# A decoder trunk on one core: scaled activations issued earlier, one more pair of columns with seven products in each gated MLP, and other times for the sums in DRAM

## The chip, the core and the metric

The kernel runs on one core of a Trainium2 chip. TensorE multiplies matrices and writes its results to PSUM; VectorE (DVE), ScalarE (ACT) and GpSimd (POOL) do the elementwise work; SyncE (SP) issues most DMA transfers, GpSimd the adding ones. Every engine has its own instruction stream, executed in the order in which the program lists it; the engines wait for one another on semaphores. The metric is the time of one execution on the device in microseconds. The kernel before took 1473.97 us (median of 3 runs, 1472.92 to 1474.12).

## The reference

One batch of 512 positions of width 1024 passes through two layers. Each layer has a mixer (layer 0: a gated short convolution beside differential attention; layer 1: stick-breaking attention), a cross-attention into 256 memory tokens, and a gated MLP. All of it is in float32. The change touches the gated MLP, shown here with its norm:

```python
def rmsnorm(x, g):
    xf = x.astype(jnp.float32)
    y = xf * lax.rsqrt(jnp.mean(xf * xf, axis=-1, keepdims=True) + EPS)
    return (y * g.astype(jnp.float32)).astype(x.dtype)

def conv_ffn(h, w_up, w_conv, w_down):
    """Gated MLP with causal depthwise width-3 conv between up-projection and activation."""
    u = causal_dwconv(h @ w_up, w_conv)
    gate, val = jnp.split(u, 2, axis=-1)
    return (jax.nn.silu(gate) * val) @ w_down

# in every layer l
x = x + conv_ffn(rmsnorm(x, norm_ffn[l]), ffn_w_up[l], ffn_conv[l], ffn_w_down[l])
```

`w_up` is 1024 x 5632 (2816 gate columns and 2816 value columns), `w_down` 2816 x 1024.

## The kernel before

Activations lie transposed, 128 features on the partitions by 512 positions, so the width of 1024 is eight chunks. Every float32 operand of a product is carried as two parts, `hi` (rounded) and `lo` (the remainder), and a product is three matmuls: hi x hi, hi x lo and lo x hi. The helper `split` makes the parts: a copy on ScalarE for `hi`, a subtraction on VectorE for `lo`.

Weights come in groups (`weight_groups`), loaded in order by SP (`loads`, `halved_loads`) into three `raw` buffers, and are split (`prep`, `prep_halved`) into five `hi` and five `lo` buffers. For groups in `LOW` the low part is made otherwise: ScalarE writes the negated rounded weights and a DMA issued by GpSimd adds the weights to them (`add_dma`).

The up-projection goes in 22 pairs `U0` to `U21`: 128 gate columns with the 128 value columns that belong to them. The order of pairs and of the parts of the down-projection is `FFN_ORDER`: U0 to U7, then D(0,0), U8, D(0,1), U9, U10 and so on; U13, U14, U15 and U16 follow one another.

- Pairs below `UP_SCALED` = 6 multiply activations that carry the norm's gain but not yet its per-position factor; their results are scaled when they leave PSUM (`up_done`: a multiplication by `rrow`), because the factor is known only later.
- Pairs from 6 on use the scaled activations that `fold` (line 1467) makes once `rrow` is known: four quarters, each with two scaled chunks (`N["S"]`) and their sums and differences (`N["T"]`).
- A plain pair is 8 chunks x 2 halves x 3 matmuls of 512 columns. A pair in `SEVEN` (line 40) is computed by `lin_halved` (line 804) as a 2 x 2 block product with seven block products in place of eight: 7 x 4 x 3 matmuls of 256 columns, with sums of the weight blocks before and sums of the products afterwards, on VectorE. Each product goes through the four quarters of the fold in turn.

The sums of the weight blocks for pairs in `SUMMED` (line 42) are made in DRAM by `sums_in_dram` (line 658): SP copies the group of 1 MB within DRAM, then GpSimd issues three adding DMAs, each of which waits for the one before. The table names, for each pair, the group after whose end the sum is spawned. `halved_loads` then loads the pair's four tiles `a`, `d`, `b` and `c`, two of them from DRAM sums.

Every result passes through `done` streams: evacuation from PSUM, `conv3` (line 1154: one ScalarE pass and two VectorE steps), the activation, the product of gate and value, and the split for the down-projection.

The order of every engine's instructions is fixed when the program is written, by a planner (`Issue.run`, line 337). Each piece of work is a stream with a priority (a lower number goes first). The planner keeps a modelled time for every engine, takes the engine on which something can start first, and among the streams that can start there at that time picks the one of the lowest number. The priorities that matter here: 0.5 for the norm's chunks, `SUM` (line 151) for the norm's sums of squares, 1.0 for the `done` streams, `FOLD` (line 153, used in line 1585) for the fold, 3.0 for the preparation of weights, 6.0 for the sums in DRAM, 10 and up for the matmuls. Fixed numbers of buffers bound how far a stream can run ahead: three PSUM accumulators (`acc`), two each of `sc` and `tr` and one `pv`, six `c` buffers in SBUF.

Of the kernel before, what the change touches and what calls it, by code (L numbers as in the profile page):

```python
# [36 lines left out]

UP_SCALED = 6
FFN_ORDER = [('u', 0), ('u', 1), ('u', 2), ('u', 3), ('u', 4), ('u', 5), ('u', 6), ('u', 7), ('d', 0, 0), ('u', 8), ('d', 0, 1), ('u', 9), ('u', 10), ('d', 0, 2), ('u', 11), ('u', 12), ('d', 0, 3), ('u', 13), ('u', 14), ('u', 15), ('u', 16), ('d', 1, 0), ('u', 17), ('d', 1, 1), ('u', 18), ('d', 1, 2), ('u', 19), ('u', 20), ('d', 1, 3), ('u', 21), ('d', 2, 0), ('d', 2, 1)]
SEVEN = {0: (7, 8, 9, 10, 11, 12, 13, 14, 15, 16, 17, 18, 19, 20, 21), 1: (7, 8, 9, 10, 11, 12, 13, 14, 15, 16, 17, 18, 19, 20, 21)}  # L40

SUMMED = {0: {7: 'A1', 8: 'A1', 9: 'A2', 10: 'A2', 11: 'EO0', 12: 'EO0', 13: 'EO1', 14: 'KV1_0', 15: 'KV3_0', 16: 'Q0_0', 17: 'Q0_0', 18: 'Q1_0', 19: 'XO0_0', 20: 'XO0_0', 21: 'XO1_0'}, 1: {7: 'U17_0', 8: 'U19_0', 9: 'U21_0', 10: 'SQK0', 11: 'SQK0', 12: 'SV0', 13: 'SQK1', 14: 'SQK2', 15: 'SV1', 16: 'SQK3', 17: 'Q0_1', 18: 'Q1_1', 19: 'XO0_1', 20: 'XO1_1', 21: 'U1_1'}}


def weight_groups():
# [57 lines left out]
GROUPS = weight_groups()  # L103
GN = {g[0]: i for i, g in enumerate(GROUPS)}

LOW = {GN[n] for n in ('U2_0', 'U2_1', 'U3_0', 'U3_1', 'U4_0', 'U4_1', 'U5_0', 'U5_1', 'U6_0', 'U6_1')}
LOW7 = {GN[n] for n in ()}
ADDED = {GN[f"U{j}_{l}"]: GN[after] for l in SUMMED for j, after in SUMMED[l].items()}
HALVED = {GN[f"U{j}_{l}"] for l in SEVEN for j in SEVEN[l]}
NSLOT = [len(g[3]) * len(g[4]) * P // SLOT for g in GROUPS]  # L110
# [37 lines left out]

POW_WAIT = 0.0

PREP_FIRST, SUM_FIRST, SUM = 0.45, 3.2, 1.5

FOLD = 1.4

SUMS = 6.0
PE_RATE, PE_FIX = 2400.0, 0.0133
# [88 lines left out]
class Issue:  # L245
# [8 lines left out]
    def spawn(self, gen, prio):  # L254
        self.seq += 1
        self.streams.append(Stream(gen, prio, self.seq))
# [133 lines left out]
def trunk(ctx: ExitStack, tc: tile.TileContext, xT: bass.AP, memT: bass.AP, wts: bass.AP, par: bass.AP, outT: bass.AP):  # L390
# [36 lines left out]
    def act(out, in_, func=AF.Copy, scale=1.0, bias=None, accum=None):  # L427
        out, in_ = vw(out), vw(in_)
        scale, bias, accum = vw(scale), vw(bias), vw(accum)
        d = (0.051 if in_.psum() else 0.093) + in_.n() / 1200.0  # L430
        d += 0.093 * (isinstance(scale, V) + (bias is not None)) + 0.2 * (accum is not None)
        kw = {}
        if bias is not None:
            kw["bias"] = _raw(bias)
        if accum is not None:
            kw["accum_out"] = _raw(accum)
        if func == AF.Copy and scale is not None and not isinstance(scale, V) and scale == 1.0:
            def fn():
                return nc.scalar.copy(out=out.ap, in_=in_.ap)  # L439
        else:  # L440
            def fn():
                return nc.scalar.activation(out=out.ap, in_=in_.ap, func=func, scale=_raw(scale), **kw)  # L442
        return Op("ACT", d, [in_, scale, bias], [out, accum], fn)
# [299 lines left out]
    def prep(groups):  # L743
        for gi in groups:
# [3 lines left out]
            for s in range(NSLOT[gi]):  # L748
# [9 lines left out]
                else:  # L758
                    yield Until(lambda: (gi, s) in raws)
                    raw = raws[gi, s]  # L760
                    yield act(hi, raw)
                    if gi in LOW:
                        yield act(lo, raw, scale=-1.0)
# [699 lines left out]
    def ffn(l, xin, xout, last):  # L1463
# [40 lines left out]
        def up_done(j):  # L1504
            def done(m, ps):
                gate = m % 2 == 0
                u = ps
                if j < UP_SCALED:
                    u = yield AL(pC)
                    yield Until(lambda: "rrow" in N)  # L1510
                    yield tt(u, ps, N["rrow"], ALU.mult)
                    free(ps)
                t = yield AL(pG)
                yield from conv3(u, f"ffn_conv{l}", j if gate else 22 + j, 44, t)
                free(u)
                if gate:
                    yield act(t, t, AF.Silu)
                    gate_t[j] = t
                    F["silu", l] = F.get(("silu", l), 0) + 1
                else:  # L1520
                    yield Until(lambda: j in gate_t)
                    yield tt(t, t, gate_t[j], ALU.mult)
                    free(gate_t[j])
                    if 4 <= j < 16 or j > 19:
                        q = pHS if j < 16 else pG
                        hi, lo = yield [AL(q, F32R), AL(q, F32R)]
                        o, w = (hi, lo), (hi, lo)
                    else:
                        y = yield AL(pH, F32R, (P, 2, S))
                        o, w = (y[:, 0, :], y[:, 1, :]), (y,)  # L1530
                    yield from split(o[0], o[1], t)
                    free(t)
                    own[j] = w
                    acts[j] = o
            return done

        def up(j):
            done = up_done(j)
            if j in SEVEN[l]:
                acc = yield AL(aACC)  # L1540
# [43 lines left out]

        spawn(fold(), FOLD)
        for step in FFN_ORDER:
# [283 lines left out]
```

## Time and profile before

| what | before |
|---|---|
| median of 3 runs | 1473.97 us |
| profiled execution | 1473.73 us |
| its span, first to last instruction | 1471.9 us |
| TensorE busy | 1465.0 us |
| VectorE / ScalarE / GpSimd busy | 1113.1 / 810.7 / 168.5 us |
| moved by DMA | 243.41 MB |

The span lies 1.83 us below the profiled execution's time. The profile's matmuls overlap and their ends are modelled, so the distance between two starts tells how long one takes, not its duration. "Idle before" is the time in which an engine had nothing to execute just before an instruction, and the arrow names what ended it. A DMA's time to landing runs from its issue to the last byte. In the trace `L492` is the helper that records matmuls, `L454` the one for elementwise work on two tensors, `L439` and `L442` ScalarE's copies and activations, `L462` VectorE's scaled additions, `L501` SP's DMAs and `L508` the adding DMAs of GpSimd (POOL).

### The profile page before, as it was taken

The numbers are of one execution on the slowest core, as the hardware profiler recorded it, in microseconds if no ns is written. First come the engines' busy times: TensorE is split into PE (matmuls) and PEld (weight loads), VectorE is DVE, ScalarE is ACT, GpSimd is POOL, SyncE is SP. The second block draws the span as 40 slices with busy tenths as digits, with TensorE's granted clock in tenths as the row PEclk, the third lists the DMA queues.
The fourth block names the chain that finished last, engine by engine and source line by source line (L and its number), as shares of the span: only waits on it lengthen the run. The fifth ranks groups of instructions, "written<-read, shape, count | busy, mean of one in ns | idle before, by whom it ended". The sixth has DMA issues, their size and how long they took to land.

```text
span 1471.9 us, 21459 instructions
## 1 busy us (share of the span) xinstructions
PE 1465.0 (100%) x8048; PEld 1272.2 (86%) x8048; DVE 1113.1 (76%) x1891; ACT 810.7 (55%) x1335; POOL 168.5 (11%) x249
## 2 busy tenths in 40 slices
PE   9999999999999999999999999999999999999998
PEld 8888888888889999999888888888888889999897
DVE  7689766665798788867687989967656996888683
ACT  6576546453675445444477877855535854545341
POOL 3212121211210000000111111001101300000000
PEclk9999999999999999999999999999999999999999
DMA  6128898967784445658465463453547954455351
GB/s 237 58 86 243 224 264 269 255 169 161 178 177 143 144 151 170 200 169 227 158 154 147 122 187 79 137 178 107 148 126 219 224 149 128 144 159 184 117 165 57
DMA packets 86088, 243.41 MB, mean 165 GB/s; under 512 B 8064, under 2 KB 8576, under 8 KB 85504
## 3 DMA queue, kind: packets, MB, share of 16 engines
q1 hardware_dynamic: 63744, 200.09, 40.2%
q0 software_dynamic: 22240, 41.95, 17.6%
q8 instruction: 63, 1.03, 0.3%
q14 instruction: 41, 0.34, 0.1%
HBM read 239.91 MB, written 65.01 MB: 207 GB/s over the span
## 4 chain that ended last, share of the span: by engine, by line
PE 95%; DVE 2%; ACT 2%; DMA 1%; issue 1%; SPq 0%; DVEq 0%; ACTq 0%
PE acc L492 67%; PE sc L492 13%; PE pv L492 6%; PE tr L492 6%; PE tr L496 3%; DVE lo L454 0%; ACT h L439 0%; DMA raw<-wts 0%; ACT g L442 0%; DMA x<-xT 0%; DVE g L1619 0%; DVE h L454 0%; DVE g L454 0%; DVE c L454 0%; ACT pt L439 0%
## 5 line engine op out<-in xcount | busy, mean ns | idle before, releaser
L492 PE MATMUL acc<-hs,hi 128*128 128x512 f32 x1568 | 493.7, 392 | 0.0
L439 ACT CAST hi<-raw 128x1024 fp32r<-128x1024 f32 (+1 forms) x294 | 303.3, 1038 | 211.1 <-PE acc L492 79.8
L454 DVE TENSOR_TENSOR lo<-raw,hi 128x1024 fp32r<-128x1024 f32 (+1 forms) x274 | 328.7, 1205 | 90.7 <-ACT hi L439 89.5
L492 PEld LDWEIGHTS acc<-hs,hi 128*128 128x128 f32 x1568 | 292.4, 188 | 57.7
L492 PE MATMUL acc<-hs,lo 128*128 128x512 f32 x784 | 307.5, 392 | 0.0
L492 PE MATMUL acc<-hi,hs 128*128 128x512 f32 x544 | 175.4, 395 | 0.3 <-ACT hs L442 0.3
L492 PEld LDWEIGHTS acc<-hs,lo 128*128 128x128 f32 x784 | 147.3, 188 | 28.7
L492 PE MATMUL acc<-h,hi 128*128 128x512 f32 (+1 forms) x600 | 170.2, 368 | 0.0
L454 DVE TENSOR_TENSOR x<-x,acc 128x512 f32<-128x512 f32 (+1 forms) x105 | 71.2, 680 | 71.4 <-PE acc L492 71.1
L492 PEld LDWEIGHTS acc<-h,hi 128*128 128x128 f32 x600 | 108.2, 189 | 18.1
L462 DVE SCALAR_TENSOR_TENSOR g<-c,pp,g 128x511 f32<-128x511 f32 (+1 forms) x168 | 116.9, 745 | 2.5 <-ACT g L442 2.4
L492 PEld LDWEIGHTS acc<-hi,hs 128*128 128x128 f32 x544 | 100.9, 188 | 20.3 <-ACT hs L442 0.6
L492 PE MATMUL acc<-h,lo 128*128 128x512 f32 (+1 forms) x300 | 109.5, 368 | 0.0
L492 PE MATMUL acc<-lo,hs 128*128 128x512 f32 x272 | 106.8, 393 | 0.0
L492 PE MATMUL acc<-y,hi 128*128 128x512 f32 (+1 forms) x280 | 74.2, 346 | 0.0
L508 POOL DMA_DIRECT2D dr<-wts x30 | 27.4, 913 | 392.1 <-DMA dr<-wts 385.6
L442 ACT ACTIVATE g<-c,pp 128x512 f32<-128x512 f32 x84 | 58.1, 719 | 19.1 <-DVE c L454 18.9
L454 DVE TENSOR_TENSOR g<-g,g 128x512 f32<-128x512 f32 (+2 forms) x112 | 62.9, 568 | 5.0 <-ACT g L439 2.0
L492 PEld LDWEIGHTS acc<-h,lo 128*128 128x128 f32 x300 | 56.6, 189 | 9.4
L442 ACT ACTIVATE g<-sc,rq 128x128 f32<-128x128 f32 (+7 forms) x128 | 61.2, 537 | 5.4 <-PE sc L492 4.9
L508 POOL DMA_DIRECT2D dr<-dr x60 | 50.3, 848 | 115.3 <-DMA dr<-wts 70.1
L492 PEld LDWEIGHTS acc<-lo,hs 128*128 128x128 f32 x272 | 51.2, 188 | 10.0
(241 smaller groups left out, 2672.1 us busy)
## 6 DMA issues: line engine op xcount, KB each, us to landing
raw<-wts SPq DMA_DIRECT2D x226, 512.0 KB, 4.2
raw<-dr SPq DMA_DIRECT2D x60, 512.0 KB, 3.7
dr<-wts POOLq DMA_DIRECT2D x30, 512.0 KB, 6.1
dr<-dr POOLq DMA_DIRECT2D x60, 256.0 KB, 4.7
lo<-wts POOLq DMA_DIRECT2D x20, 512.0 KB, 7.8
raw<-wts SPq DMA_DIRECT2D x38, 256.0 KB, 3.1
x<-xT SPq DMA_DIRECT2D x16, 256.0 KB, 4.7
raw<-memT SPq DMA_DIRECT2D x4, 512.0 KB, 4.5
```

The costliest lines, as they stand in the source:

```text
L439: return nc.scalar.copy(out=out.ap, in_=in_.ap)
L442: return nc.scalar.activation(out=out.ap, in_=in_.ap, func=func, scale=_raw(scale), **kw)
L454: lambda: _ve(eng).tensor_tensor(out=out.ap, in0=in0.ap, in1=in1.ap, op=op))
L462: lambda: nc.vector.scalar_tensor_tensor(out=out.ap, in0=in0.ap, scalar=_raw(scalar), in1=in1.ap, op0=op0, op1=op1))
L492: lambda: nc.tensor.matmul(out.ap, lhsT.ap, rhs.ap, start=start, stop=stop))
L496: return Op("PE", 0.109, [in_, ident_v], [out], lambda: nc.tensor.transpose(out.ap, in_.ap, ident_v.ap))
L508: lambda: nc.gpsimd.dma_start(out=out.ap, in_=i, accum_op=ALU.add, max_dma_last_dim=2048))
```

## The change

Three things change, by tables and priorities alone; no function is edited.

- Pair 6 of both layers joins `SEVEN` and leaves `LOW`. It needs a sum in DRAM too, so it enters `SUMMED`: 32 sums in place of 30.
- The fold's priority goes from 1.4 to 0.8 and the norm sums' from 1.5 to 0.7, so both stand ahead of the `done` streams at 1.0.
- The sums in DRAM are spawned after other groups. Layer 0's pairs 18 to 21 come after pairs 7 to 10 of the first gated MLP; layer 1's pairs 6 to 14 after its pairs 11 to 20; layer 1's last four after pairs 8 to 11 of the second gated MLP. None is spawned in the stick-breaking layer.

```diff
 UP_SCALED = 6
-SEVEN = {0: (7, 8, 9, 10, 11, 12, 13, 14, 15, 16, 17, 18, 19, 20, 21), 1: (7, 8, 9, 10, 11, 12, 13, 14, 15, 16, 17, 18, 19, 20, 21)}
-SUMMED = {0: {7: 'A1', 8: 'A1', 9: 'A2', 10: 'A2', 11: 'EO0', 12: 'EO0', 13: 'EO1', 14: 'KV1_0', 15: 'KV3_0', 16: 'Q0_0', 17: 'Q0_0', 18: 'Q1_0', 19: 'XO0_0', 20: 'XO0_0', 21: 'XO1_0'}, 1: {7: 'U17_0', 8: 'U19_0', 9: 'U21_0', 10: 'SQK0', 11: 'SQK0', 12: 'SV0', 13: 'SQK1', 14: 'SQK2', 15: 'SV1', 16: 'SQK3', 17: 'Q0_1', 18: 'Q1_1', 19: 'XO0_1', 20: 'XO1_1', 21: 'U1_1'}}
+SEVEN = {0: (6, 7, 8, 9, 10, 11, 12, 13, 14, 15, 16, 17, 18, 19, 20, 21), 1: (6, 7, 8, 9, 10, 11, 12, 13, 14, 15, 16, 17, 18, 19, 20, 21)}
+SUMMED = {0: {6: 'A1', 7: 'A1', 8: 'A2', 9: 'A2', 10: 'EO0', 11: 'EO0', 12: 'EO1', 13: 'KV1_0', 14: 'Q0_0', 15: 'Q0_0', 16: 'Q1_0', 17: 'XO0_0', 18: 'U7_0', 19: 'U8_0', 20: 'U9_0', 21: 'U10_0'}, 1: {6: 'U11_0', 7: 'U12_0', 8: 'U13_0', 9: 'U14_0', 10: 'U15_0', 11: 'U16_0', 12: 'U17_0', 13: 'U18_0', 14: 'U20_0', 15: 'Q0_1', 16: 'Q1_1', 17: 'XO0_1', 18: 'U8_1', 19: 'U9_1', 20: 'U10_1', 21: 'U11_1'}}
...
-LOW = {GN[n] for n in ('U2_0', 'U2_1', 'U3_0', 'U3_1', 'U4_0', 'U4_1', 'U5_0', 'U5_1', 'U6_0', 'U6_1')}
+LOW = {GN[n] for n in ('U2_0', 'U2_1', 'U3_0', 'U3_1', 'U4_0', 'U4_1', 'U5_0', 'U5_1')}
...
-PREP_FIRST, SUM_FIRST, SUM = 0.45, 3.2, 1.5
-FOLD = 1.4
+PREP_FIRST, SUM_FIRST, SUM = 0.45, 3.2, 0.7
+FOLD = 0.8
```

## Prediction

> **What bounds the kernel now.** I read the page first, then the busy time by stretch, then the starts of the matmuls. Lines of the page of before: the span, the busy time of TensorE, the chain that ended last, and the issues of plain weight loads.
>
> ```profile
> span 1471.9 us, 21459 instructions
> ...
> PE 1465.0 (100%) x8048; PEld 1272.2 (86%) x8048; DVE 1113.1 (76%) x1891; ACT 810.7 (55%) x1335; POOL 168.5 (11%) x249
> ...
> PE 95%; DVE 2%; ACT 2%; DMA 1%; issue 1%; SPq 0%; DVEq 0%; ACTq 0%
> ...
> L454 DVE TENSOR_TENSOR lo<-raw,hi 128x1024 fp32r<-128x1024 f32 (+1 forms) x274 | 328.7, 1205 | 90.7 <-ACT hi L439 89.5
> ...
> raw<-wts SPq DMA_DIRECT2D x226, 512.0 KB, 4.2
> ```
>
> TensorE is on the chain for 95% of the span and idle for 6.9 us of it (1471.9 - 1465.0). Every microsecond that its instruction stream loses is therefore won, and every wait that it gains is lost. Where the 6.9 us lie, by stretch (busy time of each engine, number of instructions, clock, DMA share, GB/s):
>
> ```profile
> core 0: us, PE busy (x) PEld busy (x) DVE busy (x) ACT busy (x) POOL busy (x), PEclk, DMA share, GB/s
> 110.00:160.00 50.00, 49.47 (x256) 41.50 (x255) 42.68 (x122) 28.60 (x68) 12.43 (x13) 1.00 0.85 217
> 211.00:254.00 43.00, 43.00 (x201) 35.51 (x200) 29.56 (x42) 24.60 (x43) 7.32 (x9) 1.00 0.85 260
> 390.00:440.00 50.00, 50.00 (x222) 41.38 (x222) 46.20 (x78) 37.05 (x53) 8.42 (x7) 1.00 0.85 187
> 440.00:500.00 60.00, 60.00 (x372) 54.26 (x371) 44.70 (x67) 28.61 (x39) 0.00 (x0) 1.00 0.40 128
> 740.00:800.00 60.00, 59.31 (x298) 49.53 (x297) 48.23 (x79) 42.53 (x85) 11.06 (x29) 1.00 0.65 160
> 800.00:850.00 50.00, 49.68 (x262) 41.30 (x261) 49.25 (x83) 43.76 (x86) 8.13 (x28) 1.00 0.43 114
> ```
>
> TensorE has no gap at all where the first gated MLP begins (390 to 500 us), at the full granted clock (1.00). What gaps the change could remove lie in 110:160 (0.53 us) and in the stick-breaking layer, 740:800 and 800:850 (0.69 + 0.32 us). Most of the rest stands at the start and the end of the span. So the change can win little except by shortening the stream itself.
>
> **The change part by part.** *Pair 6 with seven products.* Starts of matmuls on TensorE (start, us busy, what, count), at the borders of steps of both gated MLPs:
>
> ```profile
> 440.39 0.62 PE L492 MATMUL acc<-y,hi 128*128 128x512 f32 x2
> ...
> 451.27 0.40 PE L492 MATMUL acc<-y,hi 128*128 128x256 f32 x2
> ...
> 461.34 0.63 PE L492 MATMUL acc<-h,hi 128*128 128x512 f32 x2
> ...
> 585.58 0.40 PE L492 MATMUL acc<-y,hi 128*128 128x256 f32 x2
> ...
> 1185.88 0.62 PE L492 MATMUL acc<-y,hi 128*128 128x512 f32 x2
> ...
> 1196.76 0.40 PE L492 MATMUL acc<-y,hi 128*128 128x256 f32 x2
> ...
> 1206.83 0.63 PE L492 MATMUL acc<-h,hi 128*128 128x512 f32 x2
> ```
>
> The plain pair 6 runs from 440.39 to 451.27, 10.88 us for its 48 matmuls (2 halves x 8 chunks x 3) of 512 columns: 227 ns each. Pair 7, already with seven products, runs from 451.27 to 461.34, 10.07 us for 84 matmuls (7 x 4 x 3) of 256 columns: 120 ns each. Layer 1 has the same differences (1196.76 - 1185.88 and 1206.83 - 1196.76). The edit turns one 10.88 into a 10.07 in each layer: 2 x 0.81 = **1.62 us less**, all on the path.
>
> The Trainium skill ("TensorE: Matmul & The Clock Gate", section Back-to-back issue gap) gives a sustained 81 ns per matmul of 128 columns and 131 ns of 512; an estimate on the line between them is 98 ns for 256, by which 84 x 98 = 8.2 us would replace 48 x 131 = 6.3 us and each pair would lose 1.9 us. The trace disagrees with both figures (227 and 120 ns), so the measured difference stands.
>
> *What pair 6 costs on the other engines.* So far its low parts are made by ScalarE and an adding DMA; now VectorE makes them: three of 1.2 us (the page's row) and a half one, and it also combines the products with seven sums. Rows of VectorE in pair 7's turn:
>
> ```profile
> 457.56 0.69 DVE L454 TENSOR_TENSOR sq<-raw,sq 128x512 fp32r<-128x512 f32 x1
> ...
> 461.55 0.42 DVE L454 TENSOR_TENSOR c<-sc,c 128x256 f32<-128x256 f32 x1
> 461.88 0.41 DVE L454 TENSOR_TENSOR c<-c,sc 128x256 f32<-128x256 f32 x1
> ```
>
> That is 3 x 1.2 + 0.7 + 7 x 0.33 = 6.6 us more of VectorE per layer. In 440:500 VectorE is idle for 60 - 44.70 = 15.3 us, which hides it; the results are wanted only when the down projection that starts at 461.34 reaches its seventh and eighth chunk. I take nothing; were the cover gone, it would cost up to 6.6 us in each layer. ScalarE trades four passes over 1024 columns for three and two small ones: nothing. POOL loses two adding DMAs for low parts, and SP issues four loads in place of two.
>
> *The fold.* The scaled activations (`fold`) get priority 0.8, ahead of the 1.0 of the evacuations and convolutions of pairs 0 to 5. Pair 6 needed only the plain scaled chunks, one after another; with seven products its first product needs all four quarters, the last some 1.1 us after its start (three quarters of a 1.44 us product, 10.07 / 7), at about 441.5. Where each quarter starts now on VectorE, and its last write:
>
> ```profile
> 390.70 0.74 DVE L462 SCALAR_TENSOR_TENSOR c<-x,pp,rrow 128x512 f32<-128x512 f32 x1
> ...
> 409.63 1.41 DVE L462 SCALAR_TENSOR_TENSOR c<-x,pp,rrow 128x512 f32<-128x512 f32 x2
> ...
> 422.46 0.74 DVE L462 SCALAR_TENSOR_TENSOR c<-x,pp,rrow 128x512 f32<-128x512 f32 x1
> ...
> 435.98 1.40 DVE L462 SCALAR_TENSOR_TENSOR c<-x,pp,rrow 128x512 f32<-128x512 f32 x2
> ...
> 449.68 0.68 DVE L454 TENSOR_TENSOR rrow<-c,pt 128x512 fp32r<-128x512 f32 x1
> ```
>
> It ends at 450.36, 0.9 us before pair 7; for the new pair 6 that is 8.9 us late. The quarters take 18.9, 12.8, 13.5 and 14.4 us, though a quarter has only some 5 us of VectorE work (two scalings of 0.7, four low parts of 0.7, four sums of 0.4: 5.8 by durations). What stretches them is the pairs' work between, which the new priority puts behind. Bounds: at 5.8 us each the fold ends at 414; at 12.8 each it ends at 442, just late. I take an end near 425, so **nothing**. The displaced work is two scaled copies and four convolution steps a pair, held by the three accumulators and six `c` buffers; VectorE has 3.8 us of idle time in 390:440, so the backlog is pushed into the 15.3 us after 440.
>
> The norm sums (`SUM`, 0.7) move ahead of the same evacuations: one addition of about 0.7 us in front of another, neither of them last before the statistics. I take nothing.
>
> *The sums in DRAM.* 32 in place of 30. By stage, before and after: even layer and first cross-attention 15 and 12; first gated MLP 3 and 13; stick-breaking layer 7 and 0; second cross-attention 4 and 3; second gated MLP 1 and 4. So the stick-breaking layer loses its traffic. Its largest gap, at 779.38, goes back to a weight load. From the chain of waits (start, us, what), the waits of ScalarE and of POOL's queue, and the gap:
>
> ```profile
> 769.95 6.26 DMA raw<-wts
> ...
> 776.23 1.05 ACT L439 CAST hi<-raw 128x1024 fp32r<-128x1024 f32 x1 [2.72 <-DMA raw<-wts]
> ...
> 769.09 0.89 POOL L508 DMA_DIRECT2D dr<-wts  x1 [9.18 <-DMA dr<-wts]
> ...
> 779.38 0.55 PE tr L496 x3
> ...
> PE tr L496 <- DVE pt L454: 0.7, 1, 0.7
> ```
>
> The load took 6.26 us against the page's median of 4.2, beside a sum's add that POOL issued at 769.09; ScalarE held a copy and the cast of `pt` behind it. Without the sum it comes up to 2.1 us earlier, more than the 0.7 us that TensorE waited. Bounds: 0 (another operand is late next) and 1.0 (all the idle time of both stretches). I take **0.7 us less**.
>
> Sum, against the profiled execution's own time (1473.73, of which 1.83 lie outside its span): 1473.73 - 1.62 - 0.7 = 1471.4. The median of the runs is 0.24 above that execution: **1471.7**. If the 0.7 stays, 1472.4.
>
> **The rivals.** *Slower: the first gated MLP becomes bound by its weight loads (0.22).* Loads of the dense stretch as they are, and a stretch with one sum (queue: packets, MB, share; then the issues with KB and median time to landing):
>
> ```profile
> q1 hardware_dynamic: 3880, 8.41, 55.1%
> ...
> raw<-wts SPq DMA_DIRECT2D x8, 512.0 KB, 3.7
> ...
> q0 software_dynamic: 560, 1.05, 21.2%
> ...
> raw<-wts SPq DMA_DIRECT2D x7, 512.0 KB, 5.7
> ```
>
> The first two rows are of 560:610, the others of 660:692. Loads: 55.1% of 50 us for 8.41 MB is 3.28 us of all DMA engines per MB; a pair of 3.5 tiles (1.84 MB) needs 6.0 us. A sum: its adds 21.2% of 32 us = 6.8 us, its 1.05 MB copy 3.4 us. With a sum after every pair a pair's time of 10.07 us meets 16.2 us of DMA. Pairs 13 to 16 follow each other without a down projection: 4 x 6.1 = 24.5 us too much. Against that stands the lead of the weights, as here (cast and its low part on VectorE; the product that uses them starts at 585.58):
>
> ```profile
> 575.19 1.05 ACT L439 CAST hi<-raw 128x1024 fp32r<-128x1024 f32 x1 [1.18 <-DMA raw<-wts]
> 577.18 1.22 DVE L454 TENSOR_TENSOR lo<-raw,hi 128x1024 fp32r<-128x1024 f32 x1
> ```
>
> 585.58 - 578.40 = 7.2 us. The rest is hidden as far as adds fall behind the loads, since the sums are wanted much later: each that does takes 6.8 us out. With two of four behind, TensorE waits 24.5 - 7.2 - 13.6 = 3.7 us, with one 10.5; the middle, 7.1, gives 1471.7 + 7.1 = 1478.8, and it decides from 5.3 us up (below that the run is not slower by over 0.2%). Loads already land 2 us later beside one sum, and the copies stand on SP ahead of the loads. Against it: 211:254 runs at a DMA share of 0.85 with no gap on TensorE, and the adds wait for one another on POOL. The forecast needs two and a half sums' adds to fall behind.
>
> On which queue gives way, the Trainium skill ("DMA: Bandwidth & Descriptors", section Queues, rings and completion order) says that an engine takes turns between the queues that have work; by that the loads would not go first, which speaks for this rival, and the 5.7 us agree.
>
> *The fold is early, but not enough (0.10).* At the pace of its third quarter, 13.5 us, it ends at 390.7 + 54 = 444.7, 3.2 us after it is wanted, in each layer: 1471.7 + 6.4 = 1478.1.
>
> *The priority does nothing (0.03).* The fold ends at 450.4 as now: 8.9 us in each layer, 1489.5.
>
> *Faster (0.07).* All the gaps named above close (0.53 + 0.69 + 0.32) beside the 1.62: 1470.8.
>
> *Short matmuls cost more than they save (0.01).* Seven products lose once 256-column matmuls stand over 10.88 / 84 = 130 ns apart. If the weight loads set the pace at their own duration,
>
> ```profile
> L492 PEld LDWEIGHTS acc<-hs,hi 128*128 128x128 f32 x1568 | 292.4, 188 | 57.7
> ```
>
> 188 ns, a pair would take 84 x 0.188 = 15.8 us, and the time would be 1473.97 - 0.7 + 2 x 4.9 = 1483.1. Pair 7 in both layers, at 120 ns, speaks against it. This is the case in which the figures of the Trainium skill's TensorE page, named above, would hold.
>
> **How the numbers follow.** The forecast with its variant at 1472.4 has 0.57, its own range 1470.9 to 1473.4. About 0.2%, 2.95 us, is what a measurement of this kernel tells from no change. Faster than 1471.0: the faster rival and a little of the forecast's low end, 0.10. Slower than 1476.9: most of the load rival (0.17), about half of the late fold (0.05) and 0.04 of the two small ones, 0.26. The same: 0.64. The range, 1470.4 to 1479.2, takes in the load rival up to a little over its middle and the late fold, and leaves out its upper bound, the fold unmoved and a larger gain.
>
> **What would show it.** Right: pair 6 starts with 256-column matmuls in both layers and takes about 10.1 us with no gap before it; the last fold write ends before 440; TensorE has no idle time between 390 and 740, and less than now in 740:800. The load rival would show as waits of TensorE, or of ScalarE's casts, for `raw` between 540 and 640 with loads landing at 6 us or more; the late fold as a gap just ahead of the first 256-column product of each layer, ended by VectorE; a backlog of VectorE as a gap inside the first down projection. A gap of more than 5 us at any of these makes the prediction wrong.

## The result and the profile after

| | before | changed |
|---|---|---|
| median, in runs side by side | 1473.47 us (1472.92 to 1474.12) | 1484.49 us (1482.69 to 1485.9) |
| ratio, 95% interval | 1 | 1.0074 [1.0056, 1.0091] |
| profiled execution, its span | 1473.73, 1471.9 us | 1482.69, 1480.9 us |

The changed kernel is slower by 0.74%, 11.0 us by the medians. The forecast of 1471.7 us is missed and the time lies above the range. The profiled execution is the fastest of the four; in it the span is 9.0 us longer than in the one before, and that is what the traces can account for. Lines of the page of the changed kernel: span, busy times, and the chain that ended last, by engine.

```profile
span 1480.9 us, 21638 instructions
...
PE 1466.2 (99%) x8120; PEld 1276.6 (86%) x8120; DVE 1120.9 (76%) x1913; ACT 811.2 (55%) x1337; POOL 167.6 (11%) x251
...
PE 89%; DMA 4%; DVE 4%; ACT 2%; issue 1%; SPq 0%; DVEq 0%; ACTq 0%
```

TensorE's share of the chain falls from 95% to 89%, and DMA's rises from 1% to 4%, though TensorE is busy nearly as long as before (1466.2 against 1465.0): its idle time grew from 6.9 to 14.7 us. Where, by stretch (busy time of each engine, clock, DMA share, GB/s):

```profile
core 0: us, PE busy (x) PEld busy (x) DVE busy (x) ACT busy (x) POOL busy (x), PEclk, DMA share, GB/s
440.00:500.00 60.00, 60.00 (x413) 56.06 (x412) 46.30 (x70) 28.26 (x38) 5.11 (x6) 1.00 0.73 213
560.00:600.00 40.00, 33.03 (x253) 32.42 (x252) 30.97 (x50) 19.02 (x26) 7.57 (x9) 0.91 1.00 292
600.00:640.00 40.00, 39.65 (x245) 35.66 (x244) 29.15 (x44) 17.79 (x23) 6.23 (x8) 1.00 0.96 268
740.00:800.00 60.00, 60.00 (x295) 50.20 (x295) 44.70 (x75) 39.54 (x77) 6.69 (x26) 1.00 0.22 71
```

Pair 6 and the following stretch to 500 us have no gap. The stick-breaking layer's 740:800 is full (59.31 before). Seven microseconds are missing in 560:600, where the DMA engines are busy all the time. Here pairs 13 to 16 of the first gated MLP follow one another; the stops come in pair 14 (0.28 us), pair 15 (2.44) and pair 16 (4.25), each at the second of the seven products, and grow from pair to pair. A fourth, of 0.35 us, comes in pair 17. The starts of TensorE's matmuls: the borders of pairs 6 and 7, and then the places where it stopped (in brackets the idle time before and what ended it; pair 16's first product, `acc`, ends at 589.9 and its second, `sc`, starts at 594.15).

```profile
440.68 0.40 PE L492 MATMUL acc<-y,hi 128*128 128x256 f32 x2
...
460.83 0.40 PE L492 MATMUL acc<-h,hi 128*128 128x512 f32 x1
...
579.57 0.51 PE L492 MATMUL sc<-y,hi 128*128 128x256 f32 x2 [2.44 <-DVE c L454]
...
589.63 0.28 PE L492 MATMUL acc<-h,lo 128*128 128x256 f32 x1
594.15 0.80 PE L492 MATMUL sc<-y,hi 128*128 128x256 f32 x2 [4.25 <-DVE c L454]
...
596.88 1.48 PE L492 MATMUL pv<-kl,sq 128*128 128x256 f32 x6
...
599.30 0.40 PE L492 MATMUL tr<-kl,hi 128*128 128x256 f32 x2
```

Pairs 6 and 7 together take 460.83 - 440.68 = 20.15 us, where they took 461.34 - 440.39 = 20.95: 0.80 less, as forecast. The stops end with "DVE c": TensorE is not waiting for a weight. The product that stands still writes to an `sc` buffer of PSUM, of which there are two, and it is freed when VectorE has added its old content into `c`, which takes two instructions (`c<-c,sc` and `c<-sc,c`). Why VectorE was late shows in its own timeline, beside the chain of waits for the same stretch.

```profile
588.16 1.23 DVE L454 TENSOR_TENSOR lo<-raw,hi 128x1024 fp32r<-128x1024 f32 x1 [2.34 <-ACT hi L439]
...
592.21 1.22 DVE L454 TENSOR_TENSOR lo<-raw,hi 128x1024 fp32r<-128x1024 f32 x1 [1.89 <-ACT hi L439]
593.35 0.41 DVE L454 TENSOR_TENSOR c<-c,sc 128x256 f32<-128x256 f32 x1
593.68 0.42 DVE L454 TENSOR_TENSOR c<-sc,c 128x256 f32<-128x256 f32 x1
```

```profile
568.57 7.96 DMA raw<-dr
...
576.54 1.06 ACT hi L439
...
577.62 1.23 DVE lo L454
...
580.18 1.14 DVE lo L454
...
581.34 9.77 DMA raw<-dr
...
591.13 1.05 ACT hi L439
...
592.21 1.22 DVE lo L454
593.43 0.39 DVE c L454 x2
```

A load of a DRAM sum took 9.77 us to land. ScalarE cast it, VectorE made its low part, and only then came the additions from `sc`, whose data had been ready: the engine's order is fixed, and the low part stood ahead. The stopped product itself uses the same weight tile as the product before it, and the late tile (`c` of pair 16, by the order of the loads) is first used by the sixth product, which starts at 602.17. So one late load stopped TensorE through VectorE's order, before any product needed what it brought.

The chain also shows why the stops grow. A load is issued when a low part frees one of the three `raw` buffers (the low part of 580.18 ends at 581.32, the load goes out at 581.34), so a low part that comes late makes the next load late in turn. The chain goes from load to cast to low part to load, and no matmul is on it from 556 to 600 us. An estimate: a buffer is held for a tile's landing, its cast (1.05 us) and its low part (1.22). With the landing times of 560:610, 5.8 us for `a`, 7.6 for `b` and `c` and 4.9 for the half tile `d` (cast and low part 1.3), a pair's four loads hold 34.0 us of buffer time, 11.3 us with three buffers, more than the pair's 10.07; with those of before (3.7, 3.6 and 2.8) it is 7.3 us. Pairs 14, 15 and 16 took 10.6, 12.8 and 16.7 us to the start of what follows. No run changed the number of buffers.

The DMA queues of the changed kernel in 560:610 (packets, MB, share of all DMA engines' time) and the issues (KB, median us to landing; q0 carries the adds, q1 the loads and copies):

```profile
q1 hardware_dynamic: 3661, 11.67, 63.6%
q0 software_dynamic: 1706, 3.18, 36.6%
...
raw<-wts SPq DMA_DIRECT2D x7, 512.0 KB, 5.8
...
raw<-dr SPq DMA_DIRECT2D x6, 512.0 KB, 7.6
```

Before, the same 50 us held 8.41 MB of loads at 55.1%, and plain loads landed after 3.7 us. Now copies raise the first queue to 11.67 MB and the adds of three sums (3.18 MB) take 36.6%: the two make 100.2%. The adds are slowed as well: those from one DRAM sum to another land after 7.7 us here (median), after 4.7 us in the whole kernel before.

The 9.0 us add up by the starts of the same matmuls in both traces. When pair 6 of the first gated MLP starts, the changed kernel is 0.3 us behind; pairs 6 and 7 win 0.8. The stops of pairs 14, 15 and 16 cost 0.5, 2.7 and 6.7 us, that of pair 17 costs 0.6. Between 752 us and pair 6 of the second layer it wins 0.9, in pairs 6 and 7 there another 0.8; a stop of 0.81 in the second gated MLP costs 1.0, and the rest wins 0.3. The 6.7 us of pair 16 are 4.25 of standing still and 2.3 of slow matmuls: the 24 after the stop take 599.30 - 594.15 = 5.15 us where 24 x 0.12 = 2.9 are usual. Why the median of the runs lies another 1.8 us above the profiled execution, no trace shows.

### The profile page after: what moved, and what is told of

Read it like the earlier page. It is cut to its first block, busy times and chain, and to the rows that moved or that the text cites. A ratio compares the mean times of both kernels' runs of the same rounds, so it can differ in the third digit from the quotient of the medians.

```text
span 1480.9 us, 21638 instructions
## 1 busy us (share of the span) xinstructions
PE 1466.2 (99%) x8120; PEld 1276.6 (86%) x8120; DVE 1120.9 (76%) x1913; ACT 811.2 (55%) x1337; POOL 167.6 (11%) x251
## 3 DMA queue, kind: packets, MB, share of 16 engines
q8 instruction: 64, 1.05, 0.3%
## 4 chain that ended last, share of the span: by engine, by line
PE 89%; DMA 4%; DVE 4%; ACT 2%; issue 1%; SPq 0%; DVEq 0%; ACTq 0%
PE acc L492 64%; PE sc L492 12%; PE pv L492 6%; PE tr L492 5%; PE tr L496 3%; DMA raw<-dr 2%; DMA raw<-wts 2%; DVE lo L454 1%; DVE c L454 1%; ACT hi L439 1%; DVE g L462 0%; ACT h L439 0%; ACT g L442 0%; DMA x<-xT 0%; DVE h L454 0%
## 5 line engine op out<-in xcount | busy, mean ns | idle before, releaser
L439 ACT CAST hi<-raw 128x1024 fp32r<-128x1024 f32 (+1 forms) x296 | 305.3, 1038 | 229.0 <-PE acc L492 74.1
L454 DVE TENSOR_TENSOR lo<-raw,hi 128x1024 fp32r<-128x1024 f32 (+1 forms) x280 | 336.4, 1205 | 98.9 <-ACT hi L439 97.5
L492 PE MATMUL acc<-h,hi 128*128 128x512 f32 (+1 forms) x576 | 161.8, 366 | 0.0
L462 DVE SCALAR_TENSOR_TENSOR g<-c,pp,g 128x510 f32<-128x510 f32 (+1 forms) x176 | 122.9, 745 | 2.1 <-ACT g L442 2.0
L492 PEld LDWEIGHTS acc<-h,hi 128*128 128x128 f32 x576 | 103.5, 189 | 17.0
L492 PE MATMUL acc<-h,lo 128*128 128x512 f32 (+1 forms) x288 | 104.4, 365 | 0.0
L508 POOL DMA_DIRECT2D dr<-dr x64 | 57.3, 909 | 155.1 <-DMA dr<-wts 99.6
L492 PE MATMUL acc<-y,hi 128*128 128x512 f32 (+1 forms) x256 | 65.9, 339 | 0.0
L439 ACT CAST pt<-tr 128x128 fp32r<-128x128 f32 (+2 forms) x96 | 43.1, 457 | 32.6 <-PE tr L496 31.9
```

The lines of the kernel that those rows point to most:

```text
L454: lambda: _ve(eng).tensor_tensor(out=out.ap, in0=in0.ap, in1=in1.ap, op=op))
L462: lambda: nc.vector.scalar_tensor_tensor(out=out.ap, in0=in0.ap, scalar=_raw(scalar), in1=in1.ap, op0=op0, op1=op1))
L492: lambda: nc.tensor.matmul(out.ap, lhsT.ap, rhs.ap, start=start, stop=stop))
L508: lambda: nc.gpsimd.dma_start(out=out.ap, in_=i, accum_op=ALU.add, max_dma_last_dim=2048))
```

## The experiments

The theories, by the letters that the expectations use. A: the new times of the sums make the loss. Within A, A1 says that it is VectorE's fixed order, and C that it is the adds' traffic on the DMA engines. The rivals are that the priorities or pair 6 make it, and others that an expectation names itself. Each time stands beside a median of before of 1473.5 to 1474.0 us on the same chip.

**Only the sums' times.** The kernel before, with the changed table for pairs 7 to 21, and nothing else.

```diff
-SUMMED = (as before)
+SUMMED = (as changed, without the entries of pair 6)
```

> The kernel before with nothing but the new times of the sums in DRAM for pairs 7 to 21; pair 6 stays plain and the priorities stay at 1.4 and 1.5 (30 sums). Theory A, the dense sums make the weight loads late in the first gated MLP: all of the loss comes without pair 6 and the priorities, 1473.5 + 8.5 (gaps of TensorE in 560:640 of the changed kernel) + 1.1 (layer 1) - 0.9 (gap of the stick-breaking layer) = 1482, with TensorE waiting for VectorE's sums of products around 565 to 625 and loads landing at 6 us or more. Theory B, pair 6 and the earlier fold leave VectorE behind, so that the sums of products are late: no gap in the first MLP here, 1472.6.

Measured 1485.18 us, ratio 1.0073 [1.0052, 1.0093]: the whole loss, though the four executions spread from 1478.81 to 1488.01, and the trace is of the longest. TensorE's waits in 540:640 (us in total, times, longest):

```profile
PE sc L492 <- DVE c L454: 9.1, 4, 4.3
```

It is the same kind of wait; here its four stops make 9.1 us. Neither pair 6 nor the priorities are needed for it.

**All but the sums' times.** The changed kernel with the table of before; pair 6 takes its sum after `A1` (layer 0) and `U15_0` (layer 1).

```diff
-SUMMED = (as changed)
+SUMMED = {0: {6: 'A1', 7: 'A1', ... as before}, 1: {6: 'U15_0', 7: 'U17_0', ... as before}}
```

> The changed kernel with the old times of the sums in DRAM; pair 6 needs a sum too, spawned after A1 in layer 0 and after U15_0 for layer 1. Theory A: only the shorter stream is left, 1473.5 - 1.6 = 1471.9, no gap in either gated MLP, the gap of 0.9 us in the stick-breaking layer back or moved. Theory B: the loss stays, 1480 or more, with gaps between 560 and 640.

Measured 1471.9 us, ratio 0.9990 [0.9981, 0.9999]. By stretch:

```profile
540.00:640.00 100.00, 100.00 (x695) 93.79 (x695) 81.98 (x129) 48.97 (x65) 5.09 (x6) 1.00 0.69 203
740.00:800.00 60.00, 59.78 (x302) 49.95 (x301) 49.02 (x82) 43.04 (x86) 11.24 (x31) 1.00 0.63 160
```

No gap in 540:640 at a DMA share of 0.69. Pair 6 and the two priorities are worth 1.8 us together against the median of before beside it, 1473.69 (by the interval 0.1 to 2.8), which fits the 1.62 of the first step, and the loss hangs on the sums' times alone.

**The priorities as before.** That kernel, with `FOLD` and `SUM` of before.

```diff
-SUM, FOLD = 0.7, 0.8
+SUM, FOLD = 1.5, 1.4
```

> As the run with the old times of the sums, with the priorities of before (fold 1.4, norm sums 1.5) too: pair 6 with seven products, fold not moved ahead. The prediction's step: the fold ends 8.9 us after pair 6 wants it in each layer, TensorE waits for it, 1471.9 + 17.8 = 1489.7. Rival: the planner fills the wait with other work or the fold ends earlier by itself, 1472 to 1476.

Measured 1486.41 us, ratio 1.0087 [1.0073, 1.0101], which is 14.5 us above the kernel with the old times. Around pair 6 of both layers, by stretch:

```profile
440.00:465.00 25.00, 21.31 (x146) 19.44 (x145) 19.42 (x31) 11.50 (x18) 0.00 (x0) 0.93 0.36 116
1190.00:1215.00 25.00, 21.30 (x140) 19.21 (x139) 19.41 (x32) 11.97 (x19) 0.00 (x0) 0.93 0.36 101
```

3.7 us idle in each layer, and a mean clock of 0.93, where the kernel with the old times has no gap and 1.00 in the first of these stretches. The fold's last write starts at 448.67. So without the priorities pair 6 costs 7.3 us per layer, waits and slow clock together; the next two runs say which of the two priorities makes it possible.

**Which of the two priorities.** The kernel with the old times and `SUM` alone as before; then both new priorities on the kernel before.

```diff
-SUM, FOLD = 0.7, 0.8
+SUM, FOLD = 1.5, 0.8
```

> The kernel with the old times of the sums, with the norm sums' priority back at 1.5 and the fold's left at 0.8. If the fold's priority alone keeps pair 6 from waiting, as the prediction had it: 1472, as with both. If the norm sums matter too: part of the 14.5 us that both old priorities cost, 1474 or more.

```diff
-SUM, FOLD = 1.5, 1.4
+SUM, FOLD = 0.7, 0.8
```

> The kernel before with the two new priorities alone (pair 6 plain, old times of the sums). The prediction took the displacement of the convolutions at nothing: 1473.7, no gap in either gated MLP. If the convolutions that are put behind hold PSUM accumulators or the down projection waits for its operands: 1475 or more.

Measured 1473.05 us, 0.9995 [0.9986, 1.0004], and 1473.33 us, 0.9996 [0.9987, 1.0005]. `FOLD` alone keeps pair 6 from waiting; for `SUM` no difference is shown, as its interval overlaps that of the kernel with both. In the second run no cost is shown of what the fold displaces.

**The planner told of late loads.** The changed kernel; the planner counts 4 us more to the landing of the loads of summed pairs, so that the casts and low parts come later in the engines' orders.

```diff
-end = self.dma_at + 1.0
+end = self.dma_at + 1.0 + op.land
...
-yield dma(v, src, w)
+o = dma(v, src, w)
+o.land = 4.0
+yield o
```

> The changed kernel, with the planner told that the loads of pairs with sums in DRAM land 4 us later than it thinks; the transfers are the same, the order on VectorE and ScalarE puts their casts and low parts later. Theory A1, TensorE waits because the sums of products (which free its PSUM buffers) stand in VectorE's order behind the low part of a tile that has not landed: the waits for VectorE's sums in 560:640 fall from 7.3 us to under 3, 1476 to 1478. Theory A2, the weights themselves come too late for their products whatever the order: the gaps stay at 8 us or more, 1482 to 1486.

Measured 1508.36 us, ratio 1.0242 [1.0224, 1.026]: no theory's number. TensorE's waits over the whole span:

```profile
PE tr L492 <- DVE lo L454: 9.6, 13, 1.2
PE tr L492 <- ACT hi L439: 5.2, 4, 1.3
...
PE sc L492 <- DVE c L454: 1.1, 3, 0.6
```

The wait for the sums of products went from 8.1 to 1.1 us, but the products now wait for their own weights, also in the second gated MLP. That three `raw` buffers leave no room for a plan that holds each one 4 us longer is a likely reason, but not shown. This tells little of the cause: the edit changed too much at once.

**The adds out of the stretch.** The changed kernel; the copies of layer 1's pairs 6 to 13 stay where they are, their adds wait for later groups (the last two of the down-projection, and those of the stick-breaking layer).

```diff
 # in sums_in_dram, behind the copy
+if gi in ADDS: yield Until(lambda: fin.get(ADDS[gi], 0) > 0)
```

> The changed kernel; for layer 1's pairs 6 to 13 the copy within DRAM stays where it is, between pairs 11 and 18 of the first gated MLP, and only the three adds wait until the end of that MLP and the stick-breaking layer. Theory C, the adds take the DMA engines from the loads: the gaps of TensorE in 550:640 (10.5 us in the changed kernel) fall under 2 us, 1473 to 1475, with some gap back in the stick-breaking layer. Theory D, the copies, which stand in SP's queue ahead of the loads, make them late: gaps of 7 us or more stay, 1481. Theory E, both by their bytes: 3 to 6 us stay, 1477 to 1480.

Measured 1472.62 us, ratio 0.9994 [0.9985, 1.0003]. The DMA queue in 560:610, and the issues:

```profile
q1 hardware_dynamic: 3896, 12.40, 74.1%
...
raw<-wts SPq DMA_DIRECT2D x8, 512.0 KB, 4.0
...
raw<-dr SPq DMA_DIRECT2D x6, 512.0 KB, 4.7
```

With the copies in place and no adds, loads land at 4.0 and 4.7 us, and nearly all the loss is gone; one stop of 1.1 us stays in 540:640.

**The copies out of it.** The counterpart: only the copies go, to times in the cross-attention and the first four pairs; the adds stay dense.

```diff
-yield Until(lambda: fin.get(after, 0) > 0)
+yield Until(lambda: fin.get(COPIES.get(gi, after), 0) > 0)
 # and between the copy and the adds
+yield Until(lambda: fin.get(after, 0) > 0)
```

> The changed kernel; for the same eight pairs only the copies move, to the end of the first cross-attention and pairs 0 to 3 of the first gated MLP; the adds stay between pairs 11 and 18. Theory C: the gaps in 550:640 stay at 8 us or more, 1482. Theory D: under 2 us, 1473. Theory E: 3 to 6 us, 1477 to 1480.

Measured 1481.49 us, ratio 1.0053 [1.0039, 1.0066]. The same view as of the last run:

```profile
q0 software_dynamic: 2734, 5.11, 61.2%
q1 hardware_dynamic: 3483, 7.17, 40.3%
...
raw<-wts SPq DMA_DIRECT2D x7, 512.0 KB, 6.9
...
raw<-dr SPq DMA_DIRECT2D x6, 512.0 KB, 7.2
```

The loads are about as late as with everything in place (6.9 and 7.2 us against 5.8 and 7.6), though the first queue moves 7.17 MB instead of 11.67. It does not change the copies alone: with their copies made early, 5.11 MB of adds fall into the 50 us instead of 3.18. Together the two runs say that the adds make the loss (C): copies alone bring little or none of it, adds alone most. The estimate of the buffers says the same: by the landing times of these two runs a pair's loads take 8.2 us without the adds and 11.5 without the copies. It is more than the bytes: 5.11 MB of adds take 61.2% of the 50 us, 12.40 MB of loads and copies 74.1%.

**VectorE's order.** Between pairs 11 and 20 of layer 0 the planner lets VectorE's sums of products stand ahead of low parts that could start a little earlier; once on the changed kernel, once on the one with the old times.

```diff
 # in up(j)
+if l == 0 and j in (11, 20): TOL["DVE"] = 1.2 if j == 11 else 0.05
```

> The changed kernel; between pairs 11 and 20 of layer 0 the planner may let a stream of higher priority take VectorE up to 1.2 us before it can start, so the sums of products (0.9) stand ahead of low parts of weights (3.0) that would have gone just before them. Same transfers. Theory A1 (the wait is one of order: TensorE already holds the weights, and its PSUM buffer is freed by a sum queued on VectorE behind a low part whose tile has not landed): gaps in 550:640 fall from 10.5 us to under 5, 1476 to 1479. Theory A2 (the weights are late in any order): 8 us or more stay, 1481 to 1486.

> The same edit of the order on the kernel with the old times of the sums, as a control: what the other order costs by itself. Expected 1471.9 as without it, up to 1 us more if low parts become late for their products.

Measured 1487.28 us, 1.0089 [1.0075, 1.0102], and 1479.05 us, 1.0034 [1.0021, 1.0047]. TensorE's waits in 540:640, on the changed kernel:

```profile
PE tr L492 <- DVE lo L454: 7.7, 4, 3.3
PE sc L492 <- DVE c L454: 0.8, 1, 0.8
```

The same on the kernel with old times:

```profile
PE tr L492 <- DVE lo L454: 4.1, 3, 2.1
PE sc L492 <- DVE c L454: 1.3, 2, 1.1
```

With dense adds the order decides where TensorE stops, not whether. With the other order it waits 7.7 us for weights instead of 7.3 for a PSUM buffer, and the order itself costs 1479.05 - 1471.9 = 7.2 us where the adds are sparse; the wait for weights is 4.1 us even there. Dense adds cost 1484.49 - 1471.9 = 12.6 us in the one order and 1487.28 - 1479.05 = 8.2 in the other. So A1 falls as a remedy, and the dense adds cost time in either order. How much of the 12.6 us the order adds to what the late loads alone would cost, this edit doesn't separate, since it changes the plan where no load is late as well.

**Only the four pairs in a row.** The changed kernel; the three sums that started after U13, U14 and U15 move to the stick-breaking layer.

```diff
-8: 'U13_0', 9: 'U14_0', 10: 'U15_0'
+8: 'SQK0', 9: 'SV0', 10: 'SQK1'
```

> The changed kernel with three sums moved: those after U13, U14 and U15 (layer 1's pairs 8, 9 and 10) go to SQK0, SV0 and SQK1 of the stick-breaking layer. The four pairs in a row then have one sum, after U16. Theory of the prediction's rival (the four pairs in a row are where DMA work exceeds the pairs' time): the gaps in 550:640 fall under 2 us, 1474. If instead the whole stretch from pair 11 on is too full: 4 us or more stay, 1478.

Measured 1475.39 us, ratio 1.0011 [1.0002, 1.0021]; TensorE's waits in 500:640:

```profile
PE sc L492 <- DVE c L454: 2.0, 3, 0.9
```

9.1 of the 12.6 us come back. Most of the loss is in the place that the rival named; three stops of under 1 us stay, one at 536 us and one each in pairs 14 and 15.

**Thinner sums.** Pair 6 and the priorities, with layer 0's sums at their old times and layer 1's spread: none after pairs 13 to 15 of the first gated MLP, and none in the stick-breaking layer.

```diff
+1: {6: 'U7_0', 7: 'U8_0', 8: 'U10_0', 9: 'U12_0', 10: 'U16_0', 11: 'U17_0', 12: 'U18_0', 13: 'U20_0', 14: 'Q0_1', 15: 'Q1_1', 16: 'XO0_1', 17: 'XO1_1', 18: 'U7_1', 19: 'U8_1', 20: 'U10_1', 21: 'U12_1'}
```

> The changed kernel with the sums spread: layer 0's pairs at the old times (pair 6 after A1), layer 1's pairs 6 to 13 after U7, U8, U10, U12, U16, U17, U18 and U20 (each right ahead of a down projection), the others after Q0, Q1, XO0, XO1 and U7, U8, U10, U12 of layer 1; none in the stick-breaking layer. Theory A (dense sums make the loads late): no gap in 550:640, and the stick-breaking layer's gap of 0.9 us gone: 1473.7 - 1.6 - 0.9 = 1471.2, under the run with the old times. If loads are late by a single sum beside them already: gaps of 2 us or more remain, 1473 or above.

Measured 1471.61 us (1471.19 to 1474.53), ratio 0.9984 [0.9975, 0.9993]. By stretch:

```profile
540.00:640.00 100.00, 100.00 (x697) 93.90 (x696) 81.78 (x129) 49.66 (x67) 6.75 (x8) 1.00 0.78 229
740.00:800.00 60.00, 60.00 (x303) 50.42 (x302) 49.26 (x82) 43.34 (x86) 2.93 (x20) 1.00 0.22 71
```

At a DMA share of 0.78 there is no gap in 540:640, and the stick-breaking layer's gap is closed too. This kernel is faster than both, by 0.16% of the time before, with an interval that just leaves out no change; between it and the one with all old times (0.9990) the intervals show no difference.

Not tried: a fourth `raw` buffer, which would test the estimate of the time that a buffer is held.

## Why the prediction was wrong

*The step that failed* is the weighing of the load rival: "The forecast needs two and a half sums' adds to fall behind", and I gave the rival 0.22. The adds did not give way: in 555:605, the turn of pairs 13 to 16, 3.93 MB of adds ran, 3.7 of the four sums. Beside them the loads went from 3.7 to 5.8 us and, for the sums, to 7.6, and the term that the sum put at nothing, waits for late loads, came to 10.5 us in the trace with the slow matmuls (0.5 + 2.7 + 6.7 + 0.6). The cover, "the lead of the weights" of 7.2 us, was read at the wrong place as well: it runs from a low part to the product that uses it, but TensorE stopped at a product whose weight was there, for a PSUM buffer that VectorE frees behind that low part.

That the middle of the rival's bounds, 7.1 us, lies so near the stops' 7.3 is luck. It supposed one or two of four sums fallen behind, and TensorE waiting for weights; with none behind, the same working gives 24.5 - 7.2 = 17.3 us. The measured 1484.49 lies above the rival's upper bound, 1471.7 + 10.5 = 1482.2: the slow matmuls after the long stop, the stop in the second gated MLP and what the other runs have above the profiled one were not in it. That the adds wait for one another does not make them fall behind the loads, and in the trace of before the one stretch with a sum, where loads landed at 5.7 us, spoke against it; I quoted it and still put the rival second.

The Trainium skill ("DMA: Bandwidth & Descriptors", section Queues, rings and completion order) says that a DMA engine takes turns between the queues that have work. The runs agree: loads land at 4.0 and 4.7 us with the second queue empty, at 6.9 and 7.2 with the adds of five sums in it, though the first queue carries less.

*What held.*

- Pair 6 with seven products, 1.62 us less: by the starts of the matmuls pairs 6 and 7 win 0.80 and 0.79 us, and the kernel without the new times came to 1471.9.
- VectorE's 6.6 us a layer at nothing: no gap in 440:500, where VectorE is now busy for 46.30 us.
- The norm sums at nothing: no difference shown.
- The stick-breaking layer 0.7 us less: 740:800 went from 59.31 to 60.00. The cause is not shown, and may be luck: with the sums still in that layer the row is 59.51 to 59.78 in three runs, but 60.00 in the run with the two new priorities alone and in the one with the old priorities.
- Short matmuls at 120 ns: pairs 6 and 7 together 20.15 us, twice 10.07.
- The fold, "an end near 425": its last write ends at 430.08, 5 us later than taken, but 11 us before it is wanted (about 441.5). Rows of VectorE in the changed kernel: the start of the first quarter, of the last, and the last write.

```profile
388.30 1.41 DVE L462 SCALAR_TENSOR_TENSOR c<-x,pp,rrow 128x512 f32<-128x512 f32 x2 [3.71 <-ACT rrow L439]
...
420.68 1.40 DVE L462 SCALAR_TENSOR_TENSOR c<-x,pp,rrow 128x512 f32<-128x512 f32 x2
...
429.40 0.68 DVE L454 TENSOR_TENSOR rrow<-c,pt 128x512 fp32r<-128x512 f32 x1
```

The first starts 2.4 us earlier than before, the last 15.3 us earlier. The case "The priority does nothing", 8.9 us a layer, was near what the old priorities cost, 7.3, though only 3.7 of these are idle time.

So the terms of the sum came out within 0.1 us, one of them without its cause being shown, and the sum was wrong by the term that it did not have. The range was wrong on the same step: it reached "a little over its middle" into a rival whose own bounds reached 10.5 us.

## What to carry to other kernels

Work that is "hidden in DMA" is hidden only while the stretch it moves to has DMA time left: add up, pair by pair, what the loads need and what the new transfers take. Here mean shares over 540:640 of 0.69 and 0.78 came with no gap, 0.84 (without the three sums) with 1.1 us idle and 0.97 (the changed kernel) with 7.3. Weigh transfers by their time on the engines, not by bytes, and expect those of another queue to share with the loads rather than give way. When TensorE waits for a buffer, look at what stands ahead of the freeing instruction in that engine's fixed order: a late load can stop a product that doesn't use it. And count how long a load buffer is held: when landing, cast and low part of a tile, divided by the number of buffers, come near the time in which a tile is used up, each late load makes the next one late.

## What was not expected of the hardware

After the stop of 4.25 us the granted clock was at half for the next products; after the one of 2.44 us it was not. Stretches of the changed kernel after the 2.44 us stop, and after the 4.25 us one:

```profile
581.00:589.60 8.60, 8.60 (x74) 8.60 (x73) 6.26 (x11) 3.04 (x5) 1.69 (x2) 1.00 1.09 265
594.20:598.80 4.60, 4.60 (x21) 4.60 (x22) 4.60 (x8) 3.50 (x6) 1.13 (x2) 0.50 0.79 234
```

In the second, 21 matmuls take 4.60 us, 219 ns each instead of 120. So this stop cost half as much again as its own length. The Trainium skill ("TensorE: Matmul & The Clock Gate", Part 1: The HAM clock gate) has the clock fall after an idle window of about 3.4 us, and 4.25 and 2.44 us lie on its two sides. Other stops here do not follow it by their length: the clock also fell to half after stops of 3.05 us (copies out of the stretch) and 2.66 us (the other order on the changed kernel), and stayed full after one of 2.93 (only the sums' times). In the run with the old priorities it fell, to the mean of 0.93 shown above, where the longest single stop was 1.98 us, with stops of 0.53 and 0.37 just before. Rows after the stops of 2.66 and 2.93 us:

```profile
574.30:577.70 3.40, 3.40 (x18) 3.40 (x17) 2.15 (x4) 2.14 (x3) 1.29 (x2) 0.50 0.92 198
...
591.40:595.00 3.60, 3.60 (x30) 3.60 (x31) 3.60 (x6) 1.34 (x2) 0.81 (x1) 1.00 1.21 439
```

What decides between them stays open.

Adds within DRAM are dear in DMA time: 5.11 MB took 61.2% of 50 us, 6.0 us of all DMA engines per MB, against 74.1% for 12.40 MB of loads and copies, 3.0 us per MB. Crowding does not explain it: with a single sum's adds in the same 50 us (`FOLD` at 0.8 and `SUM` as before) 1.05 MB took 14.0%, 6.7 us per MB.
